# More block-product chunks, their sums in PSUM and one operand added by a transfer, in the gated networks of a two-layer model

## The chip, the core and the metric

The kernel runs on one core of a Trainium2 chip. The metric is device time in microseconds (us) of one execution, from runs of the same program one after the other; the profile is one further execution, recorded by the hardware profiler. The engines are named as the profile names them: PE (TensorE, matmuls; PEld is its loading of the stationary operand), DVE (VectorE), ACT (ScalarE), POOL (GpSimd) and SP (SyncE, which here only issues transfers). SPq is SP's queue.

## The reference

A model of two layers over 256 tokens of width 1024, all in float32. Each layer has a gated feed-forward net, a mixer (convolution, recurrence, pooling), a cross attention and a second gated net, each followed by a layer norm. The change concerns the four gated nets:

```python
def swiglu(x, w_gate, w_up, w_down):
    return (jax.nn.silu(x @ w_gate) * (x @ w_up)) @ w_down

for l in range(DEPTH):                                    # DEPTH = 2
    h = layer_norm(ALPHA * h + 0.5 * swiglu(h, ffn1_gate[l], ffn1_up[l], ffn1_down[l]), ...)
    ...
    h = layer_norm(ALPHA * h + 0.5 * swiglu(h, ffn2_gate[l], ffn2_up[l], ffn2_down[l]), ...)
```

`w_gate` and `w_up` are 1024 x 2816, `w_down` is 2816 x 1024. The hidden width 2816 is five chunks of 512 and one of 256.

## The kernel before

**Products in three parts.** Every float32 operand is split into a high part, rounded to the matmul's format, and a low part, what is left. `split` (L60) does it: ScalarE casts (L61), VectorE subtracts (L62). A product is then three matmuls, high x high, high x low, low x high (`mm_rows`, L129). Weights are loaded as tiles of 128 x 1024 (512 KB) named `raw`, split into `whi` and `wlo`. There are six buffers of `raw` and eight each of `whi` and `wlo`, so the splits can run at most eight tiles ahead of TensorE. In chunks of 512 every matmul has 512 columns moving; line 105, in `product`, issues nearly all matmuls of the program.

**A gated net** is `ffn`. `xTh`, `xTl` hold the input, split and transposed: the tokens are two tiles of 128, the width eight tiles of 128. A *plain* chunk (`hidden`, or `first` for the first one) computes gate and up for 512 hidden units: 2 matrices x 2 token tiles x 8 width tiles x 3 matmuls = 96, from eight weight tiles. Into the PSUM tile `acc` a row's two halves are written interleaved (`product`, `halves`, `sums`): position 2c + h holds column c of half h. `activate` (ScalarE, silu) and `gated` (VectorE) read it back into the tile `sg`, of which there is one buffer (`activations`), in two instructions for each token tile (`by_two`). Then `turn` makes the product ready as an operand: four transfers deal it out over partitions (L450, tile `dealt`), VectorE transposes blocks (L453, tile `square`), and a split gives `ah` and `al`.

**A block-product chunk** (`by_seven`) takes gate and up together as the two halves of one matrix and input and weights as 2 x 2 blocks, and computes the four blocks of the result with seven block products instead of eight: 7 x 4 x 3 = 84 matmuls. The blocks of the input and their sums (`bx`) are made once per net (`blocks_of_x`). The weight blocks are `w00` (gate, upper half of the width), `w01` (up, upper), `w10` (gate, lower), `w11` (up, lower), two tiles each. `parts_of(r, plus)` adds a block to another in place (L597, VectorE) and splits the result; there are eight such additions of 128 x 1024 in a chunk and fourteen splits, since each of the seven products has an operand of its own. Each product goes to a bank of its own. VectorE sums the banks into `g`, `e` and `f` (`put`, L619), seven sums in a chunk, beside one copy by ScalarE (L625). `left` makes the last of them, applies silu and gate (L648, L649), and calls `turn`.

**The down projection** of a chunk is `both(c, 0)` and `both(c, 1)`, each 24 matmuls from two more weight tiles (`slab`), which accumulate over the chunks into four banks named `dn`. It trails the chunk: in turn c of the loop the second half of chunk c-2 and the first half of chunk c-1 are done. TensorE so runs in order: chunk c, `both(c-2, 1)`, `both(c-1, 0)`, chunk c+1.

**Which chunks.** `sevens` (L679): chunks 2 and 4 (the third and fifth, counted from zero) in three of the nets, chunk 4 alone in the first net of the first layer, in whose chunks 1 and 2 the small parameters and the memory are set up as well. Chunk 5 has 256 units and is done with the weights stationary (`last_hidden`).

**Order.** The program is traced in the order of its text; the framework's scheduler gives each engine a fixed order of instructions from it and puts in the waits. Each engine, and each engine's queue of transfers, takes its instructions strictly in that order, so an instruction that waits holds up all behind it. Weights are loaded by SP's queue. POOL's queue issues, in this program, the loads of the memory and small parameters near the start; besides that POOL computes one small power at each norm.

## Time and profile before

| | |
|---|---|
| device time, median of 3 runs | 1071.56 us (1070.53 to 1072.04) |
| the profiled execution: its span, first to last instruction | 1068.8 us |
| mean granted clock of TensorE | 0.998 of full speed |
| PE busy | 1059.3 us, 99% of the span, 5966 matmuls recorded |
| DVE busy | 946.3 us, 89% |
| ACT busy | 642.4 us, 60% |
| POOL busy | 66.4 us, 6% |
| transfers | 231.90 MB, mean 217 GB/s |

A page of the profile has an engine's busy time and its share of the span. A row of a group, of a timeline or of a chain names engine, line, operation, the tile written and the tile read, shapes and count; in a timeline the first two numbers are the start and the length of the merged instructions, and a bracket at the end is the idle time before and what ended it. In the view of windows each stretch has its length and then, for each engine, busy time and number of instructions, the granted clock, the share of the sixteen DMA engines and the rate. Consecutive instructions overlap a little on VectorE and ScalarE and much more on TensorE, so the pace is taken from start to start. Some matmul records can be missing.

### The profile page before, as it was taken

What the parts mean: (1) busy time and instruction counts of PE and PEld (TensorE: products, weight loads), DVE (VectorE), ACT (ScalarE), POOL (GpSimd) and SP (SyncE); (2) the same over time, 40 slices, a digit from 0 to 9 for tenths busy, and PEclk for the clock granted to TensorE, in tenths of its full rate; (3) what the DMA queues carried; (4) which work ended last, traced back from release to release, by engine and by line L of the source; (5) the groups of instructions that cost most, each with busy time, mean ns of one, the idle gap of its engine ahead of it and who ended that gap; (6) DMA issues with size and microseconds to landing.
All of it is one profiled execution on the core that took longest, in us unless ns stands there. A gap on an engine that the chain in (4) does not pass through costs nothing.

```text
span 1068.8 us, 16312 instructions
## 1 busy us (share of the span) xinstructions
PE 1059.3 (99%) x5966; PEld 937.7 (88%) x5966; DVE 946.3 (89%) x1318; ACT 642.4 (60%) x916; POOL 66.4 (6%) x114
## 2 busy tenths in 40 slices
PE   9999999999999999999999999999999999999997
PEld 7888888889899888888888888888898998888886
DVE  6977997998988799999799999788989787999996
ACT  7555664666557565656575557566764665656660
POOL 9700001000000000000000000010000000000000
PEclk9999999999999999999999999999999999999999
DMA  9997484755574575848675865856536665759461
GB/s 362 262 307 256 129 288 165 249 176 174 170 278 167 178 252 194 290 167 218 238 272 184 256 254 183 290 179 216 196 126 213 241 227 181 257 156 334 134 223 40
DMA packets 130895, 231.90 MB, mean 217 GB/s; under 512 B 9408, under 2 KB 48608, under 8 KB 130816
## 3 DMA queue, kind: packets, MB, share of 16 engines
q1 hardware_dynamic: 129024, 228.49, 64.8%
q0 software_dynamic: 1216, 1.20, 0.5%
q8 instruction: 47, 0.77, 0.3%
q10 hardware_dynamic: 576, 1.18, 0.3%
q14 instruction: 32, 0.26, 0.1%
HBM read 216.15 MB, written 1.05 MB: 203 GB/s over the span
## 4 chain that ended last, share of the span: by engine, by line
PE 99%; DMA 0%; DVE 0%; issue 0%; DVEq 0%
PE acc L105 65%; PE dn L105 31%; PE acc L172 1%; PE dn L923 1%; PE dn L982 0%; DMA h<-in_x_dram 0%; PE acc L491 0%; PE dn L981 0%; PE dn L971 0%; PE acc L1047 0%; PE dn L888 0%; DVE h L358 0%; DVE h L353 0%; PE dn L472 0%; DVE st L338 0%
## 5 line engine op out<-in xcount | busy, mean ns | idle before, releaser
L61 ACT CAST whi<-raw 128x1024 fp32r<-128x1024 f32 (+1 forms) x438 | 442.9, 1042 | 197.5 <-DVE raw L597 54.9
L62 DVE TENSOR_TENSOR wlo<-raw,whi 128x1024 fp32r<-128x1024 f32 (+1 forms) x438 | 515.7, 1209 | 32.6 <-ACT whi L61 29.0
L105 PE MATMUL acc<-whi,xT 128*128 128x512 f32 x1032 | 312.9, 380 | 0.0
L105 PEld LDWEIGHTS acc<-whi,xT 128*128 128x128 f32 x1032 | 195.1, 189 | 27.5
L105 PE MATMUL acc<-wlo,xT 128*128 128x512 f32 x516 | 195.6, 379 | 0.0
L105 PE MATMUL acc<-xT,whi 128*128 128x512 f32 x576 | 142.3, 383 | 0.2
L105 PE MATMUL dn<-whi,ah 128*128 128x512 f32 x346 | 131.5, 380 | 0.0
L105 PE MATMUL dn<-wlo,ah 128*128 128x512 f32 x346 | 131.2, 379 | 0.0
L105 PE MATMUL dn<-whi,al 128*128 128x512 f32 x346 | 131.2, 379 | 0.0
L105 PEld LDWEIGHTS acc<-xT,whi 128*128 128x128 f32 x576 | 104.0, 190 | 12.5 <-ACT whi L61 0.7
L105 PEld LDWEIGHTS acc<-wlo,xT 128*128 128x128 f32 x516 | 97.5, 189 | 13.8
L105 PE MATMUL dn<-whi,xT 128*128 128x512 f32 x288 | 87.9, 381 | 0.0
L105 PEld LDWEIGHTS acc<-xT,wlo 128*128 128x128 f32 x576 | 75.5, 191 | 3.9
L105 PE MATMUL acc<-xT,wlo 128*128 128x256 f32 x576 | 75.9, 275 | 0.0
L105 PEld LDWEIGHTS dn<-whi,al 128*128 128x128 f32 x346 | 65.4, 189 | 9.2
L105 PEld LDWEIGHTS dn<-wlo,ah 128*128 128x128 f32 x346 | 65.4, 189 | 9.2
L105 PEld LDWEIGHTS dn<-whi,ah 128*128 128x128 f32 x346 | 65.4, 189 | 9.1
L350 POOL TENSOR_TENSOR rs<-rs,nhalf 128x1 f32<-128x1 f32 x16 | 14.9, 930 | 833.6 <-DVE rs L346 598.1
L597 DVE TENSOR_TENSOR raw<-raw 128x1024 f32<-128x1024 f32 x56 | 66.2, 1217 | 0.4
L105 PEld LDWEIGHTS dn<-whi,xT 128*128 128x128 f32 x288 | 54.4, 189 | 7.7 <-DVE xT L62 0.3
L105 PE MATMUL dn<-wlo,xT 128*128 128x512 f32 x144 | 54.6, 379 | 0.0
L332 DVE SCALAR_TENSOR_TENSOR h<-h,dn 128x512 f32<-128x512 f32 x31 | 21.2, 683 | 32.9 <-PE dn L105 32.9
(234 smaller groups left out, 1277.5 us busy)
## 6 DMA issues: line engine op xcount, KB each, us to landing
raw<-in_ffn_up_dram SPq DMA_DIRECT2D x88, 512.0 KB, 5.3
raw<-in_ffn_down_dram SPq DMA_DIRECT2D x88, 512.0 KB, 6.6
raw<-in_ffn_gate_dram SPq DMA_DIRECT2D x84, 512.0 KB, 5.1
raw<-in_w_in_dram SPq DMA_DIRECT2D x48, 512.0 KB, 4.7
dealt<-sg SPq DMA_DIRECT2D x80, 128.0 KB, 4.7
raw<-in_ca_k_dram SPq DMA_DIRECT2D x16, 512.0 KB, 4.9
raw<-in_w_out_dram SPq DMA_DIRECT2D x16, 512.0 KB, 4.5
raw<-in_ca_v_dram SPq DMA_DIRECT2D x16, 512.0 KB, 5.3
```

Source lines behind the costliest of these rows:

```text
L61: nc.scalar.copy(hi, src)
L62: lows.append(nc.vector.tensor_tensor(lo, src, hi.bitcast(F32), op=ALU.subtract))
L105: nc.tensor.matmul(o, w, x, start=start, stop=stop)
L172: nc.tensor.transpose(pt[:, k, :], src[:, (4 * j + k) * P : (4 * j + k + 1) * P], unit)
L332: nc.vector.scalar_tensor_tensor(v, v, ALPHA / scale, sums(y[i][n]), op0=ALU.mult, op1=ALU.add, accum_out=None if junk is None else st[:, ...
L350: nc.gpsimd.tensor_tensor(rs, rs, nhalf[:, 0:1], op=ALU.pow)
L597: nc.vector.tensor_tensor(r[i], r[i], plus[i], op=ALU.add)
L923: nc.tensor.matmul(o[g, hh, :], kc[:, hh, g], x, start=True, stop=True)
```

## The change

More chunks are made by blocks: `sevens` becomes (3, 4) in the first net and (2, 3, 4) in the other three, eleven chunks for seven. Within such a chunk:

- Three of the seven block products are added up in PSUM. The second and third sums go on top of a bank that already holds a product: `run(..., more=True)` leaves out the flag that starts a bank afresh. ScalarE copies the bank's state out in between (`taken`), since the intermediate sums are needed too. VectorE's seven sums become three, `put` of `s`, `f` and `e`.
- The last operand, `w00` with `w10` added, is made by two transfers from DRAM on POOL's queue that add to the tile where it lies (`accum_op`). The block `w10` is thus read from DRAM twice. Six additions are left on VectorE.
- The product with `w10` alone comes fourth, and `both(c-2, 1)` moves into the chunk between the fifth and the sixth product, `both(c-1, 0)` ahead of `left`.
- The homes of `w00` and `w01` change places from one such chunk to the next.
- Silu times gate is one instruction over both token tiles.

In every chunk, the plain ones too, the hidden units lie in another order, so that one instruction reads a token tile's bank (`in_order`); the rows of `down` are loaded in the same order (`dealt`), and `turn` makes one split of 128 x 1024 where it made two of 128 x 512. The tag `up` has one buffer of twice the size.

```diff
-    def load(src, k0, nk, c0, ncol, fine=False):
+    def load(src, k0, nk, c0, ncol, fine=False, dealt=False):
...
-                loads.append(nc.sync.dma_start(
-                    raw[b // half][:, b % half : b % half + part, :],
-                    src[(a + b) * P : (a + b + part) * P, c0 : c0 + ncol].rearrange("(k p) c -> p k c", p=P),
-                ))
+                to = raw[b // half][:, b % half : b % half + part, :]
+                if dealt:
+
+                    c, u = divmod(a // 2, 2)
+                    at = slice(c * CHUNK + 2 * P * b, c * CHUNK + 2 * P * (b + 1))
+                    rows = src[at, c0 : c0 + ncol].rearrange("(p u) c -> p u c", u=2)[:, u, :]
+                    loads.append(nc.sync.dma_start(to[:, 0, :], rows))
+                else:
+                    loads.append(nc.sync.dma_start(
+                        to, src[(a + b) * P : (a + b + part) * P, c0 : c0 + ncol].rearrange("(k p) c -> p k c", p=P)
+                    ))
...
-    def product(o, w, x, start, stop):
+    def product(o, w, x, start, stop, more=False):
...
-        nc.tensor.matmul(o, w, x, start=start, stop=stop)
+        nc.tensor.matmul(o, w, x, start=start, stop=stop, skip_group_check=more)
...
+    def mm_rows(o, xh, xl, wh, wl, start, stop, more=False):
+        product(o, xh, wh, start, False, more)
+        product(o, xh, wl, False, False, more)
+        product(o, xl, wh, False, stop, more)
...
             def ordered(v):
-                return v.rearrange("p (a k j) -> p k a j", a=4, j=32)
-
-            def by_two(v, o):
-                o = o.rearrange("p (n a j m) -> p m n a j", n=2, a=4, m=2)
-                return [(ordered(v)[:, 2 * m : 2 * m + 2], o[:, m]) for m in range(2)]
+                return v.rearrange("p (a k j) -> p a k j", a=4, j=32)
+
+            def in_order(o):
+                return o.rearrange("p (a j k) -> p a k j", a=4, j=32)
 
             def activate(s, i, og):
-                for v, o in by_two(s[:, i, :], og):
-                    nc.scalar.activation(v, o, AF.Silu)
+                nc.scalar.activation(ordered(s[:, i, :]), in_order(og), AF.Silu)
 
             def gated(s, i, ou):
-                for v, o in by_two(s[:, i, :], ou):
-                    nc.vector.tensor_tensor(v, o, v, op=ALU.mult)
+                v = ordered(s[:, i, :])
+                nc.vector.tensor_tensor(v, in_order(ou), v, op=ALU.mult)
...
                 x = fp.tile([P, 4, NT, P], F32, tag="dealt", name="dealt", bufs=1)
                 for a in range(4):
                     nc.sync.dma_start(x[a * 32 : a * 32 + 32], s[:, :, a * P : (a + 1) * P])
+                d = fp.tile([P, NT, 4, P], F32, tag="up", name="square", bufs=1)
                 for i in range(NT):
-                    d = fp.tile([P, 4, P], F32, tag="up", name="square")
                     nc.vector.transpose(
-                        d.rearrange("p k (b r) -> p b k r", b=4), x[:, :, i, :].rearrange("p b (k j) -> p b k j", k=4)
+                        d[:, i].rearrange("p k (b r) -> p b k r", b=4),
+                        x[:, :, i, :].rearrange("p b (k j) -> p b k j", k=4),
                     )
-                    split(ah[:, :, tok(i)], al[:, :, tok(i)], d)
+                d = d.rearrange("p i k t -> p k i t")
+                split(*(y.rearrange("p k (i t) -> p k i t", i=NT) for y in (ah, al)), d)
                 return ah, al
...
-            def by_seven(c0, bx):
+            def by_seven(c0, bx, between):
...
-                w00 = block(gate, 0, pieces("spare0", "spare1"))
-                w01 = block(up, 0, pieces("lng", "lnb"))
+                homes = [("spare0", "spare1"), ("lng", "lnb")]
+                turn_of = sevens.index(c0 // CHUNK) % 2
+                w00 = block(gate, 0, pieces(*homes[turn_of]))
+                w01 = block(up, 0, pieces(*homes[1 - turn_of]))
                 w11 = block(up, 1, pieces("raw", "raw"))
                 w10 = block(gate, 1, pieces("spare2", "raw"))
...
-                def run(o, x, w):
+                def run(o, x, w, more=False):
                     for k in range(4):
                         wh, wl = w.at(k, slice(0, CHUNK))
-                        mm_rows(o, x[0][:, k, :], x[1][:, k, :], wh, wl, k == 0, k == 3)
-                def half_sum():
-                    return fp.tile([P, 4, P], F32, tag="up", name="half").rearrange("p k t -> p (k t)")
+                        mm_rows(o, x[0][:, k, :], x[1][:, k, :], wh, wl, k == 0 and not more, k == 3, more)
 
                 def put(o, a, op, b):
-                    nc.vector.tensor_tensor(halves(o), sums(a), halves(b), op=op)
+                    nc.vector.tensor_tensor(ordered(o), in_order(a), ordered(b), op=op)
                 s = activations()
-                g = [s[:, i, :] for i in range(NT)]
-                o = [acc((P, CHUNK)) for _ in range(4)]
+                ef = fp.tile([P, NT, CHUNK], F32, tag="up", name="halves", bufs=1)
+                e, f = ef[:, 0, :], ef[:, 1, :]
+
+                def taken(o, bank):
+                    nc.scalar.copy(ordered(o), in_order(bank))
+
+                o = [acc((P, CHUNK)) for _ in range(2)]
                 run(o[0], part_of_x(0, 0), parts_of(w00))
-                nc.scalar.copy(halves(g[0]), sums(o[0]))
-                run(o[2], bx[0], parts_of(w00, w01))
-                run(o[1], bx[1], parts_of(w00, w11))
-                e = half_sum()
-                put(e, o[1], ALU.add, g[0])
-                run(o[3], bx[2], parts_of(w01, w11))
-                put(g[1], o[3], ALU.add, e)
-                f = half_sum()
-                put(f, o[2], ALU.subtract, g[1])
-                put(e, o[2], ALU.subtract, e)
-                o = [acc((P, CHUNK)) for _ in range(3)]
-                run(o[0], bx[3], parts_of(w11))
-                run(o[1], part_of_x(0, 1), parts_of(w10))
-                run(o[2], part_of_x(1, 1), parts_of(w00, w10))
+                taken(s[:, 0, :], o[0])
+                run(o[1], bx[0], parts_of(w00, w01))
+                run(o[0], bx[1], parts_of(w00, w11), True)
+                for i in range(2):
+                    k = 4 + 2 * i
+                    nc.gpsimd.dma_start(
+                        w00[i], gate[k * P : (k + 2) * P, c0 : c0 + CHUNK].rearrange("(k p) c -> p k c", p=P),
+                        accum_op=ALU.add,
+                    )
+                taken(e, o[0])
+                o.append(acc((P, CHUNK)))
+                run(o[2], part_of_x(0, 1), parts_of(w10))
+                run(o[0], bx[2], parts_of(w01, w11), True)
+                put(s[:, 0, :], o[2], ALU.add, s[:, 0, :])
+                nc.scalar.activation(s[:, 0, :], s[:, 0, :], AF.Silu)
+                taken(f, o[0])
+                between()
+                put(f, o[1], ALU.subtract, f)
+                run(o[1], bx[3], parts_of(w11), True)
+                run(o[0], part_of_x(1, 1), parts_of(w00), True)
                 def left():
-                    put(e, o[0], ALU.add, e)
-                    for i in range(NT):
-                        put(g[i], o[1 + i], ALU.add, g[i])
-                    s = fp.tile([P, NT, CHUNK], F32, tag="spare2", name="sg", bufs=1)
-                    for i, u in enumerate((e, f)):
-                        v = ordered(s[:, i, :])
-                        nc.scalar.activation(v, g[i].rearrange("p (k a j) -> p k a j", a=4, j=32), AF.Silu)
-                        nc.vector.tensor_tensor(v, v, u.rearrange("p (k a j) -> p k a j", a=4, j=32), op=ALU.mult)
+                    activate(s, 1, o[0])
+                    put(e, o[1], ALU.subtract, e)
+                    nc.vector.tensor_tensor(s, s, ef, op=ALU.mult)
                     return turn(s)
...
             def slab(c, u):
-                w = load(down, c * 4 + 2 * u, 2, 0, DM)
+                w = load(down, c * 4 + 2 * u, 2, 0, DM, dealt=c < len(chunks) - 1)
                 ah, al = acts[c]
                 return w, ah[:, 2 * u : 2 * u + 2, :], al[:, 2 * u : 2 * u + 2, :]
 
 
-            sevens = (2, 4) if early is None else (4,)
+            sevens = (2, 3, 4) if early is None else (3, 4)
...
                 elif c in sevens:
-                    left = by_seven(c0, bx)
+                    left = by_seven(c0, bx, lambda: both(c - 2, 1))
...
                 if c > 0:
-                    if c > 1:
+                    if c > 1 and c not in sevens:
                         both(c - 2, 1)
+                    if c < len(chunks) - 1:
+                        both(c - 1, 0)
                     if c in sevens:
                         acts.append(left())
-                    if c < len(chunks) - 1:
-                        both(c - 1, 0)
```

The other lines of the diff give two more tiles the shape of the tag `up`.

12 lines of the change are left out of this document (4 added, 8 removed).

## The prediction

> **What bounds the kernel now.** I read the page first, for its span and the chain that ended last.
>
> ```profile
> span 1068.8 us, 16312 instructions
> PE 1059.3 (99%) x5966; PEld 937.7 (88%) x5966; DVE 946.3 (89%) x1318; ACT 642.4 (60%) x916; POOL 66.4 (6%) x114
> PE 99%; DMA 0%; DVE 0%; issue 0%; DVEq 0%
> ```
>
> The end is set by TensorE alone. VectorE is next: with 946.3 us it has 122 us to spare over the whole span, but an average does not say where. So I took the chain in order of time over the fourth-to-sixth hundred microseconds, where the second feed-forward net lies, and then the windows of its three middle chunks.
>
> ```profile
> 415.80 18.13 PE acc L105 x84
> 433.93 10.36 PE dn L105 x48
> 444.29 20.72 PE acc L105 x96
> 465.01 10.36 PE dn L105 x48
> 475.37 18.13 PE acc L105 x84
> 493.50 10.36 PE dn L105 x48
> ```
>
> ```profile
> core 0: us, PE busy (x) PEld busy (x) DVE busy (x) ACT busy (x) POOL busy (x), PEclk, DMA share, GB/s
> 415.80:444.29 28.49, 28.49 (x134) 24.91 (x133) 28.49 (x32) 18.28 (x22) 0.00 (x0) 1.00 0.75 216
> 444.29:475.37 31.08, 31.08 (x146) 27.23 (x145) 29.10 (x31) 17.06 (x21) 0.00 (x0) 1.00 0.68 248
> 475.37:503.86 28.49, 28.49 (x134) 24.96 (x133) 28.49 (x32) 20.09 (x22) 0.00 (x0) 1.00 0.68 197
> ```
>
> Columns of the first fence: start, length, what. An x84 piece is a chunk by seven block products, an x96 piece a plain one; x48 is the down projection of two half chunks. 18.13/84 and 20.72/96 both give 0.2158 us a matmul, piece follows piece without a hole, and the granted clock is 1.00: TensorE never waits here. But in both block-product chunks VectorE is busy for all 28.49 us of 28.49, and in the plain chunk between them for 29.10 of 31.08. TensorE is the bound by a hair. The VectorE timeline shows how thin it is.
>
> ```profile
> 398.83 1.23 DVE L62 TENSOR_TENSOR wlo<-raw,whi 128x1024 fp32r<-128x1024 f32 x1 [1.05 <-ACT whi L61]
> 401.20 1.18 DVE L597 TENSOR_TENSOR raw<-raw 128x1024 f32<-128x1024 f32 x1
> ...
> 410.31 0.75 DVE L440 TENSOR_TENSOR sg<-acc,sg 128x256 f32<-128x256 f32 x2
> 410.98 1.22 DVE L62 TENSOR_TENSOR wlo<-raw,whi 128x1024 fp32r<-128x1024 f32 x1
> 412.11 0.75 DVE L440 TENSOR_TENSOR sg<-acc,sg 128x256 f32<-128x256 f32 x2
> 412.78 3.49 DVE L597 TENSOR_TENSOR raw<-raw 128x1024 f32<-128x1024 f32 x3
> 416.18 5.76 DVE L62 TENSOR_TENSOR wlo<-raw,whi 128x1024 fp32r<-128x1024 f32 x5
> 421.86 1.30 DVE L453 STREAM_TRANSPOSE square<-dealt 128x512 f32<-128x512 f32 x2
> 423.08 1.18 DVE L62 TENSOR_TENSOR wlo<-raw,whi 128x1024 fp32r<-128x1024 f32 x1
> 424.18 1.28 DVE L62 TENSOR_TENSOR al<-square,ah 128x512 fp32r<-128x512 f32 x2
> 425.38 0.68 DVE L619 TENSOR_TENSOR half<-acc,sg 128x512 f32<-128x512 f32 x1
> 425.98 2.35 DVE L62 TENSOR_TENSOR wlo<-raw,whi 128x1024 fp32r<-128x1024 f32 x2
> ...
> 428.85 1.22 DVE L597 TENSOR_TENSOR raw<-raw 128x1024 f32<-128x1024 f32 x1
> 429.98 0.69 DVE L619 TENSOR_TENSOR half<-acc,sg 128x512 f32<-128x512 f32 x1
> 430.58 0.68 DVE L619 TENSOR_TENSOR half<-acc,half 128x512 f32<-128x512 f32 x1
> 431.27 3.50 DVE L62 TENSOR_TENSOR wlo<-raw,whi 128x1024 fp32r<-128x1024 f32 x3
> ```
>
> From start to start: a subtraction or addition of 128x1024 takes 1.136 us (416.18 to 421.86 for five), one of 128x512 0.60, the two transposes 1.22, the two gates of one token tile 0.67. The first weight tile of the block chunk is split at 398.83, after a wait for ScalarE, which had no free buffer: VectorE is then as far ahead as eight buffers allow, 17.0 us before 415.80. The eighth and last addition of this chunk is at 428.85, the fourteenth tile behind it at 431.27, done about 432.4. TensorE uses it from 415.80 + 6.5 x 2.59 = 432.6, the low part one matmul later. The 17 us are spent to within half a microsecond.
>
> **The change, part by part: TensorE.** A plain chunk becoming a block chunk loses 12 matmuls, 2.59 us. Four chunks: 10.36 us. The sums move into PSUM as more accumulation in matmuls that exist already; their count does not change. So with all else hidden the span is 1058.4.
>
> **VectorE per chunk.** Old block chunk: 18 splits and 8 additions at 1.136 (29.5), 7 sums and 2 gates at 0.60 (5.4), the turn 1.22 + 1.20: 37.4 us. New: two additions go to the transfers, four sums go, the two gates become one product of 128x1024, and the turn's two splits become one of 1.14: 24 x 1.136 + 3 x 0.60 + 1.14 + 2.36 = 32.6 us against TensorE's 28.49. Plain chunk: 12 x 1.136 + 1.34 + 2.42 = 17.4 old, about 17.2 new (one gate of 0.60 per token tile where two took 0.67). I cost PSUM read at a stride of four elements like the stride of two, which shows no penalty (0.60 from PSUM above, the same as from SBUF); a gain is excluded, a loss is taken in below. Per ordinary net VectorE gets 15.2 - 2 x 4.8 = 5.6 us more, TensorE 2.59 less.
>
> **The ledger of three block chunks in a row.** Start at 398.83 with the first tile of the net's third chunk; the two after it follow back to back. The worst place is the tenth tile of a chunk: ten splits and all six additions lie ahead of it, in TensorE's first 11.7 us (four and a half products). For the last of the three VectorE must by then have done 24 + 24 + 16 operations of 1.136 (72.7), the turns of four chunks (9.4), the gate of the plain chunk before (1.2), twice a difference `e` and the product (3.5) and four sums (2.4): 89.2 us, so 488.0. TensorE wants the tile at 415.80 + 2 x 28.49 + 11.66 = 484.4. Short by 3.6 us, and TensorE stands for that time. For the second chunk in a row the same list is 56.7 us, 455.5 against 455.95: just in time. So for the first net, which makes two; I put 0.5 there. With the old chunk's 37.4 us the last of three would be short by more than 10.
>
> Can the order spare it? The one thing not plainly urgent is the turn of the chunk before. But `square`, the turn's tile, and the halves `e`, `f` of the next chunk now share the single buffer of `up`: the copy of `e`, due before the fifth product, waits for the turn, and the fifth product is the one that uses tiles nine and ten. In the same way the first copy into `sg`, due within 5.18 us of the chunk's start, waits until the four transfers of the turn before have read it.
>
> ```profile
> 412.89 2.61 SPq L450 DMA_DIRECT2D dealt<-sg  x4
> ```
>
> ```profile
> DMA to landing us min/median/max: 2.9/3.1/3.1
> ```
>
> They are issued in 2.6 us and land 3.1 later, so the product may end no later than about 1.1 us before the next chunk starts (5.18 less 2.6, 3.1 and a copy of 0.6), 4.1 after the last product: silu 0.6 and product 1.14 leave 2.3 to spare. Nothing in the list can thus go behind the tenth tile. What can be won is VectorE's idle 1.05 us at 398.83, if the turn of the first chunk (9.0 us after its gate, as at 421.86 after 412.86) fell into it: 2.5 at the lower end. At the upper end VectorE also idles at hand-overs, which a shorter chunk has more of, since the eight buffers hold its splits back: 1.5 us a net, about the 1.05 above and half as much again, makes 5.1. I take 3.6, the list as it stands, as the rows between 401 and 434 have no idle time at all. Three nets: 10.8.
>
> **ScalarE's copies.** TensorE now waits in mid-chunk for a copy out of its bank: twice within one product, 2.59 us, and once, copy and difference, within 5.18. Behind a late copy stands all of TensorE.
>
> ```profile
> 418.47 1.06 ACT L61 CAST whi<-raw 128x1024 fp32r<-128x1024 f32 x1 [0.24 <-PE acc L105]
> 419.78 1.05 ACT L61 CAST whi<-raw 128x1024 fp32r<-128x1024 f32 x1 [0.25 <-PE acc L105]
> 420.73 0.58 ACT L625 COPY sg<-acc 128x512 f32<-128x512 f32 x1
> 430.18 6.74 ACT L61 CAST whi<-raw 128x1024 fp32r<-128x1024 f32 x7 [5.42 <-DVE raw L597]
> 478.81 0.58 ACT L625 COPY sg<-acc 128x512 f32<-128x512 f32 x1
> ```
>
> The same copy, not urgent today, ended at 421.31, 2.92 us after its product (418.39), and the second at 479.39, 1.43 us after. So 0 to 0.33 us for each of eleven chunks, 3.6 at most; I take 0, the second row. The cover is that ScalarE has 8 to 10 us free per chunk; a copy put behind a wait like the 5.42 would cost 2.8.
>
> **Adding transfers.** They go by POOL's queue, whose only work is a row of powers at each norm, and wait for the third split of their tile. Nothing like them is in the trace; nearest are these.
>
> ```profile
> raw<-in_ffn_gate_dram SPq DMA_DIRECT2D x84, 512.0 KB, 5.1
> m<-in_mem_dram POOLq DMA_DIRECT2D x32, 32.0 KB, 5.8
> ```
>
> From the start of the third product to that of the seventh TensorE has four products of 2.59 and half a down projection, 5.18: 15.5 us, and VectorE's lead is about alike at both ends. The split behind the landing takes ScalarE and VectorE 2.2, so a landing within 13 us is hidden. I bound it by 5.1, a plain load, and four times that, 20.4; POOL's row, where even 32 KB take 5.8, says that much of a landing does not grow with the bytes, so I take at most twice, 10.2: cost 0. The bytes, 1.05 MB a chunk, raise 197 to 216 GB/s to 234 to 253, and counted twice to 271 to 290, beside 248 that ran unhurt above at a DMA share of 0.68. The Trainium skill, "DMA: Bandwidth & Descriptors", section "Rules for kernel authors", says that an accumulating DMA reads its destination and writes it later, so that by it the bytes pass at least twice; no run shows that yet.
>
> **SP's queue.** The second block of chunk n+1 goes into the buffers of chunk n's last tiles, so its load waits for their split, and loads behind it on SP's queue too. TensorE wants it 1.3 + 5.18 + 2.59 = 9.1 us after that tile; load, addition, cast, split are 5.1 + 1.1 + 1.1 + 1.1 = 8.4. No loss, but no lead regained either. The strided down rows are as many transfers of the same size: 0.
>
> **Sum.** 1068.8 - 10.4 + 10.8 + 0.5 = 1069.7 for the span. The median of the runs, 1071.56, stands 2.8 above the profiled span: 1072.5. What is won on TensorE in three nets is handed back, and a little more; the first net gains 2.1.
>
> **Rivals.** *Hidden after all, faster:* VectorE gets to the third chunk earlier than the list has it (work of the list done before 398.83, or an entry too many), so that no more than 1.8 us, half, is short: 1061.2 with nothing short, 1066.6 with 1.8. For it: over three chunks VectorE loses 12.3 us on TensorE (97.8 against 85.5) and starts with a lead of 17, so the whole would fit. Against: the work lies in the first half of each chunk. *Hand-overs, slower:* TensorE's new waits and VectorE's idle time come on top. One mechanism: from the second chunk in a row on, the lead is so short that each late load, addition or copy shows. Price: 5.1 a net, 1.5 in the first, 0.1 us a chunk for the copies, 1.1: 1058.4 + 15.3 + 1.5 + 1.1 + 2.8 = 1079.1. It decides from 4.2 us a net (1073.7 is 0.2% above before). For it: 28.49 of 28.49 twice, and three new waits of TensorE on engines in strict order. Against: none of those rows shows VectorE idle. *Adding transfers late:* at four times a plain landing, 20 us, each chunk waits some 7 us, eleven chunks 77: 1138. For it there is only the unknown rate; against it, that the sum above stays hidden at twice. It decides from 13 us on.
>
> **Numbers.** The ledger as it stands 0.42, hidden after all 0.30, hand-overs 0.23, transfers late 0.05. About 0.2%, 2.1 us, is what a measurement of this kernel tells from no change. The ledger's own range, 2.5 to 4.4 us a net, is 1069 to 1075, half of it within 0.2%, the rest nearly all above. So faster 0.34 (the hidden case and the lower border), within 0.2% 0.22, slower 0.44. Range 1063.5 to 1079.5: most of the hidden case, and the hand-overs to their price.
>
> **What would show it.** TensorE's chain in the three chunks: pieces of x60, x24, x24, x24 without holes in the first block chunk of a net; in the third one holes of 3 to 4 us in all ahead of the fifth product, ended by the subtraction of line 62, if the ledger holds. A hole between second and third product would be a late copy, one before the seventh a late transfer. VectorE's additions should number 66 for 56, and its busy time rise by some 25 us (three times 5.2, and 9.8 in the first net) to 91% of the span. I am wrong if the third block chunk runs without holes, if the second net's first one has holes, or if VectorE idles for more than a microsecond or two inside the three.

## The result, and the profile after

Device time went from 1071.8 us to 1086.58 us (median of four runs, 1083.93 to 1087.4): a ratio of 1.0137, with a 95% interval of 1.0123 to 1.0151. The profiled execution of the changed kernel spans 1085.2 us, 16.4 more than that of the kernel before. First the page after: span, engines, chain by engine, the group of VectorE's additions, and the adding transfers on POOL's queue (the last number of that line is microseconds from issue to landing).

```profile
span 1085.2 us, 16259 instructions
PE 1059.0 (98%) x5918; PEld 927.8 (85%) x5918; DVE 969.0 (89%) x1279; ACT 669.1 (62%) x920; POOL 91.5 (8%) x136
...
PE 69%; DVE 15%; DMA 7%; issue 5%; ACT 3%; SPq 0%; DVEq 0%; ACTq 0%
...
L606 DVE TENSOR_TENSOR raw<-raw 128x1024 f32<-128x1024 f32 x66 | 78.7, 1215 | 1.7 <-DMA raw<-in_ffn_up_dram 1.6
...
raw<-in_ffn_gate_dram POOLq DMA_DIRECT2D x22, 512.0 KB, 6.4
```

The 48 matmuls that four chunks save are gone (5918 for 5966), and so is TensorE's monopoly of the chain: 69% for 99%, with VectorE at 15% and transfers at 7%. PE's busy time did not fall by the 10.36 us that 48 matmuls are worth; the windows below show more of it for the same matmuls where there are holes, 29.03 to 29.79 us for 28.49. VectorE's busy time rose by 22.7 us.

How much each chunk stands is seen from its start and the next one's. These are the windows of the three block chunks of the second net, the same stretch as in the prediction.

```profile
421.25:451.09 29.84, 29.03 (x133) 24.79 (x132) 28.46 (x28) 20.98 (x24) 1.19 (x1) 1.00 0.84 263
451.09:481.14 30.05, 29.09 (x134) 24.79 (x133) 30.01 (x30) 20.05 (x23) 2.38 (x2) 1.00 0.86 260
481.14:512.60 31.46, 29.79 (x134) 24.54 (x133) 29.97 (x30) 23.07 (x27) 2.39 (x2) 1.00 0.77 222
```

A block chunk without holes takes 28.49 us; here they take 1.35, 1.56 and 2.97 more, 5.9 in all, where 2.59 was to be won. In the third and fourth net, by the starts of their chunks, it is 6.6 and 5.9. TensorE's timeline names what ended the longest holes:

```profile
427.32 0.48 PE L112 MATMUL acc<-whi,kTh 128*128 128x512 f32 x1 [0.29 <-ACT sg L635]
...
433.29 0.48 PE L112 MATMUL acc<-whi,kTh 128*128 128x512 f32 x1 [0.52 <-ACT halves L635]
...
457.85 0.48 PE L112 MATMUL acc<-wlo,xT 128*128 128x512 f32 x1 [0.96 <-DVE wlo L62]
...
487.89 0.48 PE L112 MATMUL acc<-whi,xT 128*128 128x512 f32 x1 [1.41 <-ACT whi L61]
```

A bracket is less than what a hole costs, since the matmul ahead of a hole counts as busy beyond the usual pace and the one behind it takes longer (0.48 for 0.38). From start to start, with 0.2158 a matmul taken off, the first two holes cost 0.56 and 0.78 us, which is the first chunk's 1.35. The first chunk in a row waits for ScalarE's copies out of the bank (L635), the second and third for weight splits (L62, L61). The third chunk's 1.41 us stand behind its second product, well ahead of the tenth tile, which is wanted 11.66 us into a chunk. The first net, whose fourth chunk is new, is the worst place:

```profile
85.79:119.59 33.80, 30.45 (x134) 26.04 (x132) 33.48 (x46) 23.57 (x27) 2.45 (x2) 0.95 0.71 222
91.00:94.40 3.40, 0.13 (x1) 0.00 (x0) 3.40 (x4) 3.40 (x6) 1.20 (x1) 1.00 0.97 154
94.40:98.80 4.40, 4.31 (x12) 3.51 (x13) 4.40 (x11) 4.37 (x6) 0.00 (x0) 0.62 0.96 198
```

```profile
94.49 0.48 PE L112 MATMUL acc<-whi,kTh 128*128 128x512 f32 x1 [3.35 <-ACT sg L635]
```

Its fourth chunk takes 33.80 us, 5.31 over; the fifth takes 31.06 up to its end at 150.65. TensorE does next to nothing from 91.0 to 94.4 (0.13 us), then has a mean granted clock of 0.62 for 4.40 us, which is half for some 3.3 us and full for the rest. The Trainium skill, "TensorE: Matmul & The Clock Gate", section "Part 1: The HAM clock gate", says that an idle window of about 3.4 us takes the clock to half; these two rows are in keeping with it.

So TensorE stands 7.9 us in the first net, the half clock counted in, and 5.9, 6.6 and 5.9 in the others: 26.3, less 10.36 saved, is 15.9 of the 16.4.

### The profile page after: what moved, and what is told of

It is laid out like the page before. It is cut to its first block, busy times and chain, and to the rows that moved or that the text cites. A ratio compares the mean times of both kernels' runs of the same rounds, so it can differ in the third digit from the quotient of the medians.

```text
span 1085.2 us, 16259 instructions
## 1 busy us (share of the span) xinstructions
PE 1059.0 (98%) x5918; PEld 927.8 (85%) x5918; DVE 969.0 (89%) x1279; ACT 669.1 (62%) x920; POOL 91.5 (8%) x136
## 4 chain that ended last, share of the span: by engine, by line
PE 69%; DVE 15%; DMA 7%; issue 5%; ACT 3%; SPq 0%; DVEq 0%; ACTq 0%
PE acc L112 45%; PE dn L112 21%; DVE wlo L62 8%; DMA raw<-in_ffn_up_dram 3%; DMA raw<-in_ffn_gate_dram 3%; DVE raw L606 3%; ACT whi L61 2%; DMA dealt<-sg 1%; PE acc L179 1%; DVE square L458 1%; DVE sg L664 1%; PE dn L938 1%; DVE al L62 1%; DVE sg L445 0%; SPq L455 0%
## 5 line engine op out<-in xcount | busy, mean ns | idle before, releaser
L61 ACT CAST whi<-raw 128x1024 fp32r<-128x1024 f32 (+1 forms) x462 | 463.7, 1041 | 184.4 <-DVE raw L606 79.0
L62 DVE TENSOR_TENSOR wlo<-raw,whi 128x1024 fp32r<-128x1024 f32 (+1 forms) x462 | 542.5, 1207 | 27.2 <-ACT whi L61 24.4
L112 PE MATMUL acc<-whi,xT 128*128 128x512 f32 x872 | 268.5, 381 | 5.0 <-ACT whi L61 4.8
L112 PEld LDWEIGHTS acc<-whi,xT 128*128 128x128 f32 x872 | 164.9, 189 | 30.5 <-ACT whi L61 7.4
L112 PE MATMUL acc<-wlo,xT 128*128 128x512 f32 x436 | 165.8, 380 | 3.5 <-DVE wlo L62 3.5
L112 PEld LDWEIGHTS acc<-wlo,xT 128*128 128x128 f32 x436 | 82.4, 189 | 16.8 <-DVE wlo L62 5.4
L606 DVE TENSOR_TENSOR raw<-raw 128x1024 f32<-128x1024 f32 x66 | 78.7, 1215 | 1.7 <-DMA raw<-in_ffn_up_dram 1.6
L112 PE MATMUL acc<-whi,kTh 128*128 128x512 f32 x176 | 68.5, 389 | 5.8 <-ACT sg L635 3.8
L112 PE MATMUL acc<-wlo,kTh 128*128 128x512 f32 x176 | 67.7, 385 | 0.8 <-DVE wlo L62 0.8
L112 PE MATMUL acc<-whi,kTl 128*128 128x512 f32 x176 | 67.5, 383 | 0.0
```

The costliest lines, as they stand in the source:

```text
L61: nc.scalar.copy(hi, src)
L62: lows.append(nc.vector.tensor_tensor(lo, src, hi.bitcast(F32), op=ALU.subtract))
L112: nc.tensor.matmul(o, w, x, start=start, stop=stop, skip_group_check=more)
L606: nc.vector.tensor_tensor(r[i], r[i], plus[i], op=ALU.add)
```

## The experiments

Two theories to begin with. *VectorE's list*: three block chunks in a row ask more of VectorE than TensorE's time holds, so what counts is the number in a row and VectorE's work in it. *Copies*: the new waits of TensorE for ScalarE's copies cost by themselves, since in ScalarE's order they stand behind casts that wait for VectorE. The kernel before was run beside each kernel and gave 1070.85 to 1071.07 us; the ratios below stand against it.

**Seven chunks, and ten.** The first kernel goes back to the old number in the new form, the second does so in the first net alone.

```diff
-            sevens = (2, 3, 4) if early is None else (3, 4)
+            sevens = (2, 4) if early is None else (4,)
```

> The changed kernel with the seven block chunks of before: third and fifth in three nets, fifth in the first. Theory (VectorE's work in consecutive chunks eats the lead of the splits): with a plain chunk between, the lead is whole again, no wait for a split is left, and only the late copies of the first chunk of a row cost something, 1.3 us at most where they occur: 1072 to 1077 us. Rival (every chunk of the new form pays by itself, about 1.35 us for copies that stand behind casts): seven times 1.35 on top of before, 1081 us or more, with a hole before the third and the fifth product of every one.

```diff
-            sevens = (2, 3, 4) if early is None else (3, 4)
+            sevens = (2, 3, 4) if early is None else (4,)
```

> Changed kernel, but the first net makes only its fifth chunk by blocks, as before; ten chunks. The first net now loses 5.6 us against before where it should gain 2.6. Theory (its fourth chunk pays something of its own, 5.3 us of standing): these 5.6 us come back nearly whole, 1081 to 1082 us, the three other nets unchanged. Rival (the fifth chunk brings the wait with it wherever it stands): 1084 us or more.

Measured: 1075.73 us (1.0046, 1.0031 to 1.0061) and 1081.97 us (1.0103, 1.0088 to 1.0118). The four chunks by which the first kernel and the changed one differ cost 10.9 us where they should win 10.4, so each brings some 5 us of standing; the first net's alone costs 4.6, which is 7.2 of standing. Both times lie where the theory had them. But the first kernel is slower than before with the same seven chunks, and its only holes in the second net stand in the first block chunk:

```profile
422.54 0.48 PE L112 MATMUL acc<-whi,kTh 128*128 128x512 f32 x1 [0.36 <-ACT sg L635]
428.45 0.48 PE L112 MATMUL acc<-whi,kTh 128*128 128x512 f32 x1 [0.46 <-ACT halves L635]
```

**The homes in the first net.** There the memory is staged in the two buffers that `w00` takes until VectorE has turned it. This kernel gives `w00` the other pair.

```diff
-                turn_of = sevens.index(c0 // CHUNK) % 2
+                turn_of = (sevens.index(c0 // CHUNK) + (early is not None)) % 2
```

> Changed kernel; only the homes of the first two weight blocks change places in the first net. Theory (in the first net the home of the first block still holds the memory until VectorE has turned it, so the block is loaded about 10 us late, the splits and with them ScalarE's copy come late): the 3.5 us hole before the third product goes, and the 2 us at half clock behind it; 1081 to 1083 us. Rival (the copy is late by ScalarE's order, whatever the load): hole and time stay, 1086 to 1087 us.

Measured: 1084.96 us (1083.59 to 1086.6; ratio 1.0136, 1.0119 to 1.0153). That misses both forecasts, and the runs overlap with the changed kernel's: in the median the gain is 1.6 us. The profiles show what the home does: the hole shrinks and the clock stays full in the first net,

```profile
92.48 0.48 PE L112 MATMUL acc<-whi,kTh 128*128 128x512 f32 x1 [0.96 <-ACT sg L635]
```

and the first net's last chunk starts 2.6 us earlier (3.0 later than before instead of 5.6); TensorE stands 4.9 us in this net for 7.9. But that sets the fastest of this kernel's four runs (granted clock 0.999; 0.996 to 0.997 in the others) against a changed kernel's run at 0.997, so it is what home and half clock cost in this pair of executions, not a measured mean.

**More and less for VectorE.** One kernel drops the adding transfers, VectorE adds (22 additions more). One leaves out the two additions that make `w01` + `w11`, so the fifth product takes `w01` alone. One gives those two to GpSimd.

```diff
-                    nc.gpsimd.dma_start(
-                        w00[i], gate[k * P : (k + 2) * P, c0 : c0 + CHUNK].rearrange("(k p) c -> p k c", p=P),
-                        accum_op=ALU.add,
-                    )
...
-                run(o[0], part_of_x(1, 1), parts_of(w00), True)
+                run(o[0], part_of_x(1, 1), parts_of(w00, w10), True)
```

> Changed kernel without the adding transfers: VectorE adds the last operand itself, two more additions of 1.136 us in each of eleven chunks. Theory (VectorE's work sets the pace in consecutive chunks): in a net with three such chunks the last is short by 4.5 us more, in the first net by 2.3: 1097 to 1102 us. Rival (the transfers themselves cost, by their traffic or by landing late): 1086 us or less.

```diff
-                run(o[0], bx[2], parts_of(w01, w11), True)
+                run(o[0], bx[2], parts_of(w01), True)
```

> Changed kernel without the two additions of the lower up block to the upper one: the fifth product of each block chunk takes the upper block alone, so the hidden units of those chunks come out other than the reference's. VectorE has two operations of 1.136 us less in eleven chunks, ten urgent ones of its list less in the third chunk. Theory (VectorE's list sets the pace): nothing is short at the tenth tile any more, the holes that end with a split go, about 4.5 us a net in three nets and 2.5 in the first; the late copies stay: 1069 to 1073 us. Rival (order and handing over between VectorE and ScalarE, not the amount of work): 1080 us or more.

```diff
-                            nc.vector.tensor_tensor(r[i], r[i], plus[i], op=ALU.add)
+                            by.tensor_tensor(r[i], r[i], plus[i], op=ALU.add)
...
-                run(o[0], bx[2], parts_of(w01, w11), True)
+                run(o[0], bx[2], parts_of(w01, w11, nc.gpsimd), True)
```

> Changed kernel with those two additions done by GpSimd, which is idle, in place of VectorE. Theory (VectorE's amount of work): as with the two additions left out if GpSimd is done in time, 1069 to 1075 us. Rival (GpSimd takes much longer than 1.2 us for 128x1024 from two operands, or holds VectorE up while it reads): the fifth product waits for the addition, 1086 us or more.

Measured: 1109.54 (1.0362, 1.0346 to 1.0377), 1077.01 (1.0058, 1.0043 to 1.0073) and 1129.38 us (1.0544, 1.0526 to 1.0561). The first adds 25.8 us of additions (this is their group of it, 104.5 against 78.7) and 23.0 to the time, more than forecast. Some 4.5 of the 23.0 are TensorE's clock, granted at 0.993 of full speed in the mean for 0.997; the rest says that most of VectorE's work goes through to the end.

```profile
L606 DVE TENSOR_TENSOR raw<-raw 128x1024 f32<-128x1024 f32 x88 | 104.5, 1217 | 0.1
```

So the adding transfers, which the forecast cost at nothing, do what they are for. The second takes about 25 us from VectorE (22 x 1.136) and wins only 9.6, between its two forecasts. The first block chunk of its second net runs without a hole, though ScalarE's copies are all there; the longest hole of the second one is a copy:

```profile
419.25:447.74 28.49, 28.49 (x134) 24.95 (x133) 27.71 (x27) 19.61 (x23) 1.19 (x1) 1.00 0.82 272
```

```profile
454.16 0.48 PE L112 MATMUL acc<-whi,kTh 128*128 128x512 f32 x1 [0.86 <-ACT sg L635]
```

The third is as slow as its rival had it. The view of groups by form shows why GpSimd is no way out: 3.57 us an addition, and VectorE's own work gets slower beside it, the weight splits from 1.21 us to 1.28 and the additions left on it from 1.22 to 1.45. TensorE's granted clock falls to 0.977 besides, which is some 23 of the 43 us lost.

```profile
L606 POOL TENSOR_TENSOR raw<-raw 128x1024 f32<-128x1024 f32 x22 | 78.4, 3568 | 279.6 <-DVE raw L606 279.6
L606 DVE TENSOR_TENSOR raw<-raw 128x1024 f32<-128x1024 f32 x44 | 63.1, 1449 | 1.0 <-DMA raw<-in_ffn_up_dram 0.8
```

The Trainium skill, "SBUF — State Buffer", section "Who interferes with whom", says that a VectorE instruction with two inputs in SBUF contends with a GpSimd one that reads SBUF; the 1449 ns agree.

**Copies ahead of the casts.** The cheap cure, if copies are late only by their place in ScalarE's order: the casts of `w10` and of the down tiles are ordered behind them.

```diff
-                run(o[2], part_of_x(0, 1), parts_of(w10))
+                with tc.issue_after(kept.ins):
+                    p10 = parts_of(w10)
+                run(o[2], part_of_x(0, 1), p10)
...
-                between()
+                with tc.issue_after(kept_e.ins):
+                    between()
```

> Changed kernel; ScalarE's casts of the lower gate block are put behind the first copy out of the bank, those of the half down projection inside the chunk behind the second copy, by order alone. Theory (late copies are a cause of their own: 1.1 to 1.35 us in the first block chunk of each net, 3.5 us and 2 at half clock in the first net): they go, 3 x 1.2 + 5, so 1077 to 1080 us. Rival (VectorE sets the pace and a copy in time only moves the wait to the next split): 1084 us or more, with longer holes that end with a split.

Measured: 1098.27 us (1.0254, 1.0222 to 1.0286), 12 slower than the changed kernel: the rival's time, but not its holes, which were to end with a split. The copies are still late, now in all three chunks:

```profile
427.03 0.48 PE L112 MATMUL acc<-whi,kTh 128*128 128x512 f32 x1 [1.24 <-ACT sg L635]
...
457.62 0.48 PE L112 MATMUL acc<-whi,kTh 128*128 128x512 f32 x1 [1.34 <-ACT sg L635]
...
490.12 0.48 PE L112 MATMUL acc<-whi,kTh 128*128 128x512 f32 x1 [1.50 <-ACT sg L635]
```

Why is not shown: casts held behind copies might feed VectorE later, but its idle time ahead of the splits did not grow (25.6 us for 27.2). This tells that the order can't be mended by hand in this way, not that copies cost nothing; the next pair shows what they cost.

**Own banks, at seven chunks and at eleven.** The third, fifth and last product get a bank of their own, so no product waits for a copy just asked for; VectorE makes three sums more a chunk.

```diff
-                run(o[0], bx[1], parts_of(w00, w11), True)
+                run(o[2], bx[1], parts_of(w00, w11))
...
-                taken(e, o[0])
+                put(e, o[2], ALU.add, s[:, 0, :])
...
-                run(o[0], bx[2], parts_of(w01, w11), True)
+                run(o[0], bx[2], parts_of(w01, w11))
...
-                taken(f, o[0])
+                put(s[:, 1, :], o[0], ALU.add, e)
...
-                put(f, o[1], ALU.subtract, f)
+                put(f, o[1], ALU.subtract, s[:, 1, :])
...
-                run(o[0], part_of_x(1, 1), parts_of(w00), True)
+                run(o[2], part_of_x(1, 1), parts_of(w00))
...
-                    activate(s, 1, o[0])
+                    put(s[:, 1, :], o[2], ALU.add, s[:, 1, :])
+                    nc.scalar.activation(s[:, 1, :], s[:, 1, :], AF.Silu)
```

> The changed kernel with the old number of block chunks, seven, and with a bank of its own for the third, the fifth and the last product, so that no product waits for a copy out of its bank; VectorE gets three sums of 0.60 us a chunk more, ScalarE two copies less. Theory A (the waits for ScalarE's copies are a cost of their own wherever the copy is urgent): the 1.2 us a net that the third and fourth product of a single block chunk stood in e1_seven_chunks go, VectorE's 34.4 us a chunk stay below the 37.4 that ran without holes before: 1070.5 to 1072.5. Rival B (what stood there was VectorE's lateness, and the copy only the place where it showed): with 1.8 us more of VectorE's work a chunk the holes move to the subtractions and grow: 1076 to 1080.

> The changed kernel with its eleven block chunks, and own banks as in e9_own_banks_seven, nothing else: no product waits for a copy, VectorE has 1.8 us a chunk more. Theory (at three chunks in a row VectorE's list is the main cause, and copies cost only where VectorE has a lead): the copies' 1 to 1.2 us in the first chunk of each row go, and the third chunk is later by the 1.8 x 2.5 of the list, so nothing is won: 1085 to 1092. Rival (the copies are the main cause at eleven chunks too): below 1081.

Measured: 1071.3 us at seven (1.0003, 0.9994 to 1.0013) and 1108.64 at eleven (1.0358, 1.0343 to 1.0374). At seven the copies are thus worth 4.4 us (1075.73 less 1071.3), though VectorE has more to do; its block chunk runs whole:

```profile
416.30:444.79 28.49, 28.49 (x134) 24.88 (x133) 28.18 (x29) 21.82 (x25) 1.19 (x1) 1.00 1.03 329
```

At eleven the same edit costs 22 us, well above the forecast. The 33 sums of 0.60 make 19.8, but not all of the 22 are VectorE's: the mean granted clock is 0.987 for the changed kernel's 0.997, which over some 1100 us is about 11. Three windows and a few matmuls of TensorE's timeline of this kernel:

```profile
459.00:463.00 4.00, 2.58 (x13) 1.91 (x12) 3.99 (x5) 2.16 (x3) 0.00 (x0) 1.00 1.04 238
463.00:467.00 4.00, 3.19 (x10) 2.42 (x11) 4.00 (x6) 4.00 (x5) 0.00 (x0) 0.78 1.07 301
467.00:471.00 4.00, 4.00 (x16) 3.37 (x15) 4.00 (x5) 4.00 (x6) 0.00 (x0) 0.79 1.04 392
```

```profile
462.99 0.48 PE L112 MATMUL acc<-whi,kTh 128*128 128x512 f32 x1 [1.42 <-ACT whi L61]
464.28 0.48 PE L112 MATMUL acc<-wlo,kTh 128*128 128x512 f32 x1 [0.81 <-DVE wlo L62]
...
466.93 0.63 PE L112 MATMUL dn<-wlo,ah 128*128 128x512 f32 x1
467.36 0.63 PE L112 MATMUL dn<-whi,al 128*128 128x512 f32 x1
```

Two short waits with one matmul between them, and the matmuls then come 0.43 us apart, twice 0.2158, for some 3.4 us. The 0.78 and 0.79 are means: from 465.27 to 468.68 alone the view gives 0.50.

**The list by itself.** Every kernel so far that took the copies away gave VectorE more. The next one has own banks, the first net's homes changed, and leaves out the sums that this needs: VectorE's list is that of the changed kernel, 32.6 us a chunk, and no product waits for a copy. The one after it leaves the two additions out as well.

```diff
-                put(e, o[2], ALU.add, s[:, 0, :])
...
-                put(s[:, 1, :], o[0], ALU.add, e)
...
-                put(f, o[1], ALU.subtract, s[:, 1, :])
+                put(f, o[0], ALU.subtract, s[:, 0, :])
...
-                    put(s[:, 1, :], o[2], ALU.add, s[:, 1, :])
-                    nc.scalar.activation(s[:, 1, :], s[:, 1, :], AF.Silu)
-                    put(e, o[1], ALU.subtract, e)
+                    activate(s, 1, o[2])
+                    put(e, o[1], ALU.subtract, s[:, 0, :])
```

> The forecast's own term by itself: eleven block chunks with own banks and without waits for copies, but with VectorE's list as in the changed kernel, 32.6 us a chunk: the sums that own banks would need are left out, so the output is not the reference's. The first net's homes are changed over as in e3_first_net_homes. Theory A (the list was reckoned about right, copies and the first net's homes were the terms taken as nothing): 3 to 4.5 us of standing a net, 1 to 3 in the first: 1058.4 + 10.5 to 16 + 3.5 = 1072 to 1078, and the holes are ended by splits in the second and third chunk in a row. Rival B (the list itself was reckoned too short, copies only mark its lateness): 5.5 us and more a net stay, 1081 to 1086.

```diff
-                run(o[0], bx[2], parts_of(w01, w11))
+                run(o[0], bx[2], parts_of(w01))
```

> e13_list_alone with the two additions of the up block left out too (the fifth product takes the upper block alone), VectorE 30.3 us a chunk. Theory A (list, copies and homes are all there is): the list of the third chunk falls by 6.8 us and is in time, under 1 us of standing a net: 1061 to 1066. Rival C (a third cause, such as loads behind waiting loads on SP's queue or the eight buffers that hold the splits back, is left): 2 us and more a net, 1068 and more, with holes ended by a transfer or by a cast that waited for a buffer.

Measured: 1082.37 us (1.0109, 1.0092 to 1.0126) and 1068.55 (0.998, 0.9971 to 0.9989). The windows of the second net's three chunks, of the list alone and then of the other:

```profile
417.75:446.24 28.49, 28.49 (x133) 24.95 (x132) 27.62 (x27) 19.56 (x22) 1.19 (x1) 1.00 0.86 271
446.24:476.65 30.41, 29.29 (x133) 24.71 (x132) 30.37 (x30) 19.23 (x22) 2.38 (x2) 1.00 0.85 259
476.65:508.12 31.47, 29.28 (x133) 24.58 (x132) 29.89 (x30) 22.08 (x25) 2.38 (x2) 1.00 0.77 217
```

```profile
417.62:446.12 28.50, 28.50 (x134) 24.95 (x133) 27.76 (x27) 19.01 (x21) 1.19 (x1) 1.00 0.83 273
446.12:474.61 28.49, 28.49 (x134) 24.95 (x133) 27.32 (x27) 19.22 (x21) 2.38 (x2) 1.00 0.88 267
474.61:504.76 30.15, 29.29 (x134) 24.70 (x132) 28.45 (x28) 22.27 (x24) 2.42 (x2) 1.00 0.82 241
```

The first chunk in a row now stands for nothing, so without copies the 1.35 us there are gone; so they were with the copies kept and two additions less. With the list alone the second stands 1.92 and the third 2.98, 4.9 together (5.9 and 5.7 in the other two nets). With two additions less the second stands for nothing and the third for 1.66. Without the copies the additions thus bring 13.8 us, with them 9.6 before. The first time lies in the range of the rival, that the list itself was reckoned too short, and that is the larger cause: it stands in the second and third chunk without any copy. The first chunk's cost takes both, an urgent copy and a VectorE that is late with its additions. The last kernel still stands 1.7 to 2.3 us a net, and its time lies in the range forecast for a third cause. But its holes are ended by splits, not by transfers, and VectorE's timeline shows idle time at more hand-overs now, 2.97 us in four places:

```profile
416.21 1.23 DVE L62 TENSOR_TENSOR wlo<-raw,whi 128x1024 fp32r<-128x1024 f32 x1 [1.19 <-ACT whi L61]
417.67 3.81 DVE L62 TENSOR_TENSOR wlo<-raw,whi 128x1024 fp32r<-128x1024 f32 x3 [0.23 <-ACT whi L61]
...
435.80 1.23 DVE L62 TENSOR_TENSOR wlo<-raw,whi 128x1024 fp32r<-128x1024 f32 x1 [0.38 <-ACT whi L61]
...
449.25 3.50 DVE L62 TENSOR_TENSOR wlo<-raw,whi 128x1024 fp32r<-128x1024 f32 x3 [1.17 <-ACT whi L61]
```

So part of what leaves the list comes back as idle time. In the first net both kernels stand about 4 us in the fifth chunk; for the last one the list doesn't explain that, and it was not settled.

**The old form at eleven.** The kernel before with eleven block chunks.

```diff
-            sevens = (2, 4) if early is None else (4,)
+            sevens = (2, 3, 4) if early is None else (3, 4)
```

> The kernel of before with eleven block chunks in their old form, nothing else. Theory (VectorE's list, 37.4 us for each such chunk against 28.5 of TensorE, the lead used up in the first): each further chunk in a row costs 8.9 us less the 2.6 won, so five of them (two in three nets, where one replaces a plain chunk and one loses its rest, and one in the first): 1071.5 - 10.4 + 5 x 8.9 + 2 x 8.9 at most, 1106 to 1124 us. Rival (VectorE is not what binds): below 1095 us.

Measured: 1152.59 us (1.0761, 1.074 to 1.0783), slower than forecast. The new form is worth 66 us at that number, some 21 of them through the granted clock, which is 0.979 here; it was needed for it, and isn't enough.

**Towards a better kernel.** Own banks, `w01` + `w11` by two adding transfers more, the first net's homes changed (`added` issues two transfers as the changed kernel does for `w00`); then also an own bank for the sixth product, and one block chunk in the first net.

```diff
+                added(w01, up, 1)
...
-                run(o[0], bx[2], parts_of(w01, w11))
+                run(o[0], bx[2], parts_of(w01))
```

> The changed kernel with eleven block chunks; own banks as in e9_own_banks_seven, the up block's sum (w01 with w11 added) made by two adding transfers more, so four additions are left on VectorE, and the homes of the first net's blocks changed over as in e3_first_net_homes. VectorE per chunk 32.6 - 2.3 + 1.8 = 32.1 us. Theory (three causes: VectorE's list, urgent copies, the first net's homes): list short by about 1 us in the third chunk in a row instead of 3.6, idle hand-overs of some 2 us stay, no copies: about 3 us a net of standing, 1069 to 1074. Rival: the new adding transfers have only some 8 us from the addition that reads their tile to the cast that wants them, against 6.4 us of landing and 1.2 of issue, so each chunk waits for them ahead of the fifth product: 1078 and more.

```diff
-                run(o[1], bx[3], parts_of(w11), True)
+                put(e, o[1], ALU.subtract, e)
+                run(o[3], bx[3], parts_of(w11))
```

> As e10_own_banks_more_added, with the sixth product in a bank of its own too (in e10 it waited 1.6 to 2.2 us a net for VectorE's difference f to leave its bank, the sums standing behind the turn), one sum of 0.60 us a chunk more, and the first net with one block chunk, where its fourth chunk cost more than it won: ten block chunks. Theory (each wait of TensorE for a bank is a cost of its own): those holes go, the small ones of 0.44 and 0.71 us ahead of the fifth product and the down projection stay or grow by half a microsecond, the first net has none: 1061 + 3 x 1.2 to 2.5 + 2.8 for the runs, 1067.5 to 1072, below before or equal to it. Rival (VectorE's list is the bound, the bank only the place): the hole comes back as splits that are late by 2 us or more a net: 1072.5 to 1076.

Measured: 1077.75 us (1.0062, 1.0047 to 1.0077) and 1077.41 (1.0064, 1.0052 to 1.0077). Both miss. In the first, the wait went to the next bank: the sixth product waits for VectorE's difference `f`, which stands behind the turn and the splits.

```profile
466.99 0.45 PE L112 MATMUL acc<-whi,kTh 128*128 128x512 f32 x1 [1.82 <-DVE halves L625]
```

With that bank freed too, and one sum more a chunk on VectorE, late splits come back in the third chunk, four holes of 0.5 to 1.0 us from start to start; two of them:

```profile
477.93 0.48 PE L112 MATMUL acc<-wlo,kTh 128*128 128x512 f32 x1 [0.78 <-DVE wlo L62]
...
481.36 0.48 PE L112 MATMUL acc<-whi,kTh 128*128 128x512 f32 x1 [0.78 <-ACT whi L61]
```

No whole kernel run here beats the one before; own banks at seven chunks equal it.

## Why the prediction was wrong

The forecast was 1072.5 us with a range from 1063.5 to 1079.5; the time was 1086.58. Its likeliest case named the right bound, VectorE's list in three block chunks in a row, and mis-sized three terms. The ledger came to 5.7 us more than forecast, the copies to 1.9, the first net to 7.4: 15.0 of the 15.5 by which the span, 1085.2, exceeds the 1069.7 of the sum.

*TensorE's gain* was right: 48 matmuls fewer. *VectorE's work* was right: 66 additions, 22.7 us more busy time for about 25. Its share is 89% and not 91%, because the span grew.

*The ledger* failed in size: "the list as it stands", 3.6 us a net. Run by itself it gives 4.9, 5.9 and 5.7, 16.5 for 10.8, and the second chunk in a row, said to be "just in time", stands 1.9 us in the second net. The step that failed is to take VectorE's list as work without idle time, "as the rows between 401 and 434 have no idle time at all". VectorE's timeline of that kernel shows where it does idle:

```profile
415.95 1.22 DVE L606 TENSOR_TENSOR raw<-raw 128x1024 f32<-128x1024 f32 x1
418.36 5.77 DVE L62 TENSOR_TENSOR wlo<-raw,whi 128x1024 fp32r<-128x1024 f32 x5 [1.19 <-ACT whi L61]
...
438.12 1.23 DVE L606 TENSOR_TENSOR raw<-raw 128x1024 f32<-128x1024 f32 x1 [0.26 <-DMA raw<-in_ffn_up_dram]
```

An addition, the cast of its sum on ScalarE, the split on VectorE: when the split is VectorE's next instruction, VectorE idles for that cast, 1.19 us. With the 0.26 for a load this is 1.45 us; 3.6 and 1.45 make 5.05, beside 4.9 seen. In the other two nets 5.7 and 5.9 aren't taken apart further. With two additions less the same reckoning, 3.6 - 6.8 + 2.97, leaves nothing short at the tenth tile, and 1.66 us stand all the same: 0.4 of them in the fifth product, the rest ahead of the down projection's two tiles behind it. The ledger checked one place and not those. The case called hand-overs had 5.1 a net, near all of this, with 0.23 of the chance.

*ScalarE's copies*: "I take 0" failed. They cost 4.4 us at seven chunks, and at eleven 1.35 in the first block chunk of the three nets. The upper end, 0.33 us a chunk, came from how late the old copy is in two rows, but the old copy stands in another order, and the change moved it. The sentence beside it, that a copy behind a wait would cost 2.8, is what came, at half the size in the first chunk. ScalarE's timeline after:

```profile
420.78 5.78 ACT L61 CAST whi<-raw 128x1024 fp32r<-128x1024 f32 x6 [4.69 <-DVE raw L606]
426.68 0.59 ACT L635 COPY sg<-acc 128x512 f32<-128x512 f32 x1
```

After 4.69 us of waiting for VectorE six casts come in one go, and the copy stands behind them. That ScalarE has 8 to 10 us free in a chunk is no cover: the free time lies ahead of the wait. In the second and third chunk copy and list share one lateness: over the three ordinary nets the changed kernel stands 1.9 us more than the list alone, not 4.

*The first net*, "I put 0.5 there", failed most, with 7.9 for 0.5. The list counted what every net has, and not what the first net alone has: the memory's transposes and splits fall into the lead of its fourth chunk, and hold `w00`'s home until then. Rows of VectorE's and SP's timeline after:

```profile
72.64 0.69 DVE L62 TENSOR_TENSOR mT<-turned,mT 128x512 fp32r<-128x512 f32 x1 [0.69 <-ACT mT L61]
73.36 0.71 DVE L209 STREAM_TRANSPOSE turned<-m 128x512 f32<-128x512 f32 x1
```

```profile
69.53 0.37 SPq L590 DMA_DIRECT2D raw<-in_ffn_gate_dram  x1
...
74.10 1.94 SPq L590 DMA_DIRECT2D raw<-in_ffn_gate_dram  x2
```

The chunk starts at 85.79, so the two tiles of `w00`, its first operand, are asked for only 16 and 12 us ahead, where VectorE had the first tile of an ordinary net's block chunk split 17 us ahead. In the profile with the homes changed 3.0 of the 7.9 us are gone, this home and the half clock after it; with the copies out too 4.1 stay, which is not explained.

*Adding transfers, cost 0*, was right: they land in 6.4 us, inside the 13, no hole is ended by one, and the kernel without them is 23.0 us slower. *SP's queue* and *the strided reads* show no hole of their own: VectorE's additions waited 1.6 us for loads in the whole run, and the down loads land in 5.7 us for 6.6 before. They weren't tried alone.

Of the signs set up ahead for being wrong, "if the second net's first one has holes" came true (0.56 and 0.78 us from start to start), and a hole between second and third product, called a late copy there, was one. Idle time of VectorE inside the three came true as well: by the windows of the second net it is 2.9 us.

## What to carry to other kernels

When a second engine is within a few per cent of the bound, an engine in strict order must be listed with its idle time at each hand-over (add, cast, subtract), not by its work alone: at eleven chunks 25.8 us more of VectorE's work cost 23.0, some 4.5 of them through the clock. A wait put into the busiest engine's stream costs what stands ahead of the releasing instruction in its own engine's order, whatever that engine's average. Count the one-off work of each stage (the memory in the first net) before a common price is put on all.

## What the runs showed of the hardware

The clock fell to half for 3.4 us after waits of 1.42 and 0.81 us with a matmul between them, in the own-bank kernel at eleven chunks. The Trainium skill, "TensorE: Matmul & The Clock Gate", section "Part 1: The HAM clock gate", speaks of an idle window of 3.4 us; the measurement differs, and it decides: in the 3.41 us up to the fall (461.86 to 465.27, clock 1.00) TensorE was busy for 1.47. An adding transfer of 512 KB landed in 6.4 us, beside 5.1 for a plain load of gate weights before and 5.3 after. A GpSimd addition of two 128x1024 tiles took 3.57 us in the mean, and beside such additions VectorE's went from 1.22 to 1.45.
